# The last branch projection of a hybrid encoder block as seven half-size products per chunk of weights, its right factors made a stage earlier

## The chip, the cores and the metric

The kernel runs on one core of a Trainium2 chip. The metric is the device time in microseconds from the start to the end of one execution. TensorE is called PE here, VectorE DVE, ScalarE ACT, GpSimd POOL, SyncE SP, as the profile calls them.

## The reference, cut to what matters

One layer for two groups of tokens (256 and 512, together 768 columns) with the same weights. Three mixers (S5, differential attention, cross-attention) give three feature maps; each is projected by its own 1024x1024 matrix, gated and added; one output projection and a feed-forward network (FFN) follow.

```python
branches = jnp.stack([s5_out, diff_out.astype(x.dtype), mem_out.astype(x.dtype)], axis=2)
br = jnp.einsum('blnc,ncd->blnd', branches, w_branch[li])
gates = jax.nn.sigmoid((gl + b_gate[li]).astype(F32)).reshape(Bsz, L, N_BRANCH, D_MODEL)
merged = jnp.sum(gates * br.astype(F32), axis=2).astype(x.dtype)
x = x + merged @ w_out[li]
h2 = rmsnorm(x, ffn_norm_g[li])
g, up = jnp.split(h2 @ w_gate_up[li], 2, axis=-1)
x = x + (jax.nn.silu(g) * up) @ w_down[li]
```

The change concerns branch 1, the projection of the differential attention's output, and what is made ready for it.

## The kernel before, in words

Every float32 product is three matmuls in a reduced format (`mm3`, L748): each factor is split into a high part (ACT copies it and so rounds it) and a low part (factor minus high part, on DVE), and hi·hi, hi·lo and lo·hi are added in PSUM.

**Weights.** `WStream` (L518) streams all weights through fixed buffers: 3 raw halves of 512 KB (`wr`, loaded by SP), 4 high and 4 low tiles of 128x1024 (`wh`, `wl`). Weight block i is loaded in two halves `wr{i}_0` and `wr{i}_1`, and split while block i-1 is multiplied. A raw half is reused for the next load when all that reads it is done. For plain blocks the split is one copy on ACT (L595) and one subtraction on DVE (L601). Blocks of kind "w" (most of the FFN's gate and up weights) are split by `_split_w` (L561) for a product of 2x2 blocks in seven half-size products: POOL makes four sums S1 to S4 of the blocks A11, A12, A21, A22 of the weights (L572 to L579), and `_factor` (L547) makes the high and low parts of A11, A12, A22 and S1 to S4, 512 columns each, two factors to a tile. In one stretch of the program (L596 to L600) a low part is made without DVE: ACT writes the negated high copy and POOL issues a DMA that adds the raw weights to it (the "adding transfer").

**The stages around the change**, in the order in which they run: branch 2 (L1584), the half-GLU (L1587), branch 0 (L1618), branch 1 (L1620), output projection (`out_rows`, L1633), FFN. A branch runs over 4 chunks of 256 output channels (`branch`, L1505): weights 48 to 51 are branch 0, 52 to 55 branch 1 (its chunks 0 to 3), 56 to 59 the output projection. In a chunk there are 2 blocks of 128 channels (m) and 2 segments of tokens (256 and 512), each with 8 x 3 matmuls into a PSUM tile. Per m a gate row is loaded from DRAM by POOL (L1513) and goes through tanh on ACT (L1514); DVE multiplies PSUM by the gate (L1520) and adds it to `merged` (L1523). In branch 1 `merged` is then split into the pair `MG` (L1554, L1555), the left factor of the output projection.

The right factor of branch 1, the pair `Xd`, is loaded from DRAM (`br_scr`) and split by `load_pair` (L1561) during branch 0: eight rows, one 768-wide copy (L742) and one 768-wide subtraction (L743) each. The residual rows `x1` are loaded by POOL in branch 0 as well, from its second chunk on (`rows_in`, L1613). The output projection's PSUM tiles come from pools that are opened anew behind branch 1 (`psum`, L1622).

The source gives the instructions of all engines; the order of each engine's queue is set when the program is built, and an engine works its own queue strictly in that order.

## Time and profile before

| | us |
|---|---|
| time, median of 3 runs | 1745.99 (1744.87 to 1746.82) |
| profiled execution | 1746.11 |
| its span in the profile | 1744.3 |
| outside the span | 1.8 |
| branch 2, branch 0, branch 1: start to end on PE | 878 to 986, 1052.6 to 1119.9, 1119.9 to 1186.8 |
| output projection, from | 1186.8 |

Times in the trace are microseconds from the start of the span. A group row gives line, engine, operation, destination from sources, shape and count, then busy time and the mean of one in ns, then idle time of the engine in front of them and what ended it. A row of the windows gives start and end, length, busy time and instruction count of PE, PE's weight loads, DVE, ACT and POOL, the granted clock of PE, the share of DMA busy and GB/s. A DMA row gives destination from source, the issuing queue, count, size and median time from issue to landing.

### The profile page before, as it was taken

How to read it: one execution, taken by the hardware profiler on the slowest of the kernel's cores; microseconds unless marked ns; L12 is line 12 of the kernel's file. 1: busy time of each engine (PE TensorE's matmuls, PEld its weight loads, DVE VectorE, ACT ScalarE, POOL GpSimd, SP SyncE). 2: the span in 40 equal slices, each digit the busy share in tenths (PEclk: the TensorE clock that was granted, in tenths of full speed). 3: DMA queues.
4: the chain of work that ended last, by engine and by line, in shares of the span. 5: the costliest groups of instructions: out<-in, count | busy, mean ns of one | idle time of the engine just before them, and what ended most of it. 6: DMA issues, size and time to landing. Idle time of an engine off the chain costs nothing.

```text
span 1744.3 us, 29493 instructions
## 1 busy us (share of the span) xinstructions
PE 1731.5 (99%) x11236; PEld 1606.4 (92%) x11236; DVE 1262.6 (72%) x2353; ACT 889.4 (51%) x1868; POOL 270.1 (15%) x288
## 2 busy tenths in 40 slices
PE   9999999999999999999999999999999999999999
PEld 9999988999999999999989888888889999998887
DVE  7665749699999778887886445453598777776775
ACT  7444543776767346877775434232343333334443
POOL 0000000000000100111010002000036555541130
PEclk9999999999999999999999999999999999999999
DMA  8222736755566453745653437331312323238973
GB/s 271 74 85 91 125 120 134 187 126 141 145 158 159 122 145 93 169 91 155 169 160 106 133 116 247 118 118 61 90 62 91 109 91 109 91 110 290 252 158 96
DMA packets 209214, 234.11 MB, mean 134 GB/s; under 512 B 57832, under 2 KB 173296, under 8 KB 209072
## 3 DMA queue, kind: packets, MB, share of 16 engines
q1 hardware_dynamic: 182160, 167.49, 31.9%
q0 software_dynamic: 17440, 58.34, 15.5%
q10 hardware_dynamic: 9472, 6.39, 1.3%
q8 instruction: 89, 1.46, 0.4%
q14 instruction: 53, 0.43, 0.1%
HBM read 165.78 MB, written 41.22 MB: 119 GB/s over the span
## 4 chain that ended last, share of the span: by engine, by line
PE 96%; DVE 1%; ACT 1%; DMA 1%; issue 0%; SPq 0%; ACTq 0%; DVEq 0%
PE gl L751 4%; PE gl L753 4%; PE gl L752 4%; PE br L751 4%; PE br L752 4%; PE br L753 4%; PE gate L751 3%; PE gate L752 3%; PE up L752 3%; PE gate L753 3%; PE up L751 3%; PE up L753 3%; PE dn L753 3%; PE dn L751 3%; PE dn L752 3%; PE qk L751 3%
## 5 line engine op out<-in xcount | busy, mean ns | idle before, releaser
L595 ACT ACTIVATE wh<-wr 128x1024 fp32r<-128x1024 f32 x124 | 140.4, 1133 | 62.6 <-PE br L752 27.8
L601 DVE TENSOR_TENSOR wl<-wr,wh 128x1024 fp32r<-128x1024 f32 x82 | 108.5, 1324 | 80.8 <-ACT wh L595 79.0
L751 PE MATMUL gl<-H,wh 128*128 128x256 f32 (+1 forms) x384 | 132.2, 344 | 0.0
L753 PE MATMUL gl<-H,wl 128*128 128x256 f32 (+1 forms) x384 | 129.0, 336 | 0.0
L752 PE MATMUL gl<-H,wh 128*128 128x256 f32 (+1 forms) x384 | 128.7, 335 | 0.0
L599 POOL DMA_DIRECT2D wl<-wr x42 | 36.6, 872 | 506.1 <-ACT wl L598 486.8
L751 PE MATMUL qk<-wh,H 128*128 128x256 f32 x384 | 108.1, 282 | 0.0
L752 PE MATMUL qk<-wl,H 128*128 128x256 f32 x384 | 107.8, 281 | 0.0
L753 PE MATMUL qk<-wh,H 128*128 128x256 f32 x384 | 107.1, 279 | 0.0
L752 PE MATMUL dn<-wld,dxh 128*128 128x512 f32 x231 | 89.6, 389 | 0.0
L751 PE MATMUL dn<-whd,dxh 128*128 128x512 f32 x231 | 89.6, 389 | 0.0
L753 PE MATMUL dn<-whd,dxl 128*128 128x512 f32 x231 | 88.9, 389 | 0.0
L753 PEld LDWEIGHTS gl<-H,wl 128*128 128x128 f32 x384 | 72.0, 188 | 8.1
L752 PEld LDWEIGHTS gl<-H,wh 128*128 128x128 f32 x384 | 72.3, 188 | 7.2
L751 PEld LDWEIGHTS gl<-H,wh 128*128 128x128 f32 x384 | 72.3, 188 | 6.8
L557 ACT ACTIVATE wh_S<-ws 128x512 fp32r<-128x512 f32 x70 | 41.1, 625 | 65.2 <-PE up L752 36.8
L753 PEld LDWEIGHTS qk<-wh,H 128*128 128x128 f32 x384 | 72.4, 188 | 0.6
L751 PEld LDWEIGHTS qk<-wh,H 128*128 128x128 f32 x384 | 72.4, 188 | 0.6
L752 PEld LDWEIGHTS qk<-wl,H 128*128 128x128 f32 x384 | 72.3, 188 | 0.5
L558 DVE TENSOR_TENSOR wl_S<-ws,wh_S 128x512 fp32r<-128x512 f32 x70 | 57.9, 851 | 15.9 <-ACT wh_S L557 15.9
L1292 DVE TENSOR_REDUCE nm<-sc 128x1 f32<-128x512 f32 (+1 forms) x96 | 56.6, 596 | 17.6 <-PE sc L1287 16.8
L1294 ACT ACTIVATE p<-sc,nm 128x512 f32<-128x512 f32 (+1 forms) x96 | 58.8, 615 | 14.1 <-DVE nm L1292 13.6
(477 smaller groups left out, 6004.2 us busy)
## 6 DMA issues: line engine op xcount, KB each, us to landing
wr<-in_w_in_dram SPq DMA_DIRECT2D x48, 512.0 KB, 4.9
wr<-in_w_gate_up_dram SPq DMA_DIRECT2D x44, 512.0 KB, 3.6
wl<-wr POOLq DMA_DIRECT2D x42, 512.0 KB, 5.4
wr<-in_w_branch_dram SPq DMA_DIRECT2D x24, 512.0 KB, 4.8
glr<-gl_scr POOLq DMA_DIRECT2D x24, 384.0 KB, 4.0
hid_scr<-fa SPq DMA_DIRECT2D x11, 768.0 KB, 6.5
wr<-in_w_mem_kv_dram SPq DMA_DIRECT2D x16, 512.0 KB, 4.2
wr<-in_w_in_dram SPq DMA_DIRECT2D x32, 256.0 KB, 3.8
```

The lines of the kernel that those rows point to most:

```text
L557: self.nc.scalar.activation(f(hi), src, AF.Copy)
L558: self.nc.vector.tensor_tensor(out=f(lo), in0=src, in1=f(hi).bitcast(F32), op=ALU.subtract)
L595: self.nc.scalar.activation(hi, r, AF.Copy)
L599: self.nc.gpsimd.dma_start(lo, r.bitcast(F32R), accum_op=ALU.add)
L601: self.sub.tensor_tensor(out=lo, in0=r, in1=hi.bitcast(F32), op=ALU.subtract)
L751: pe.matmul(ps, wh, xh, start=start, stop=False, **kw)
L752: pe.matmul(ps, wh, xl, start=False, stop=False, **kw)
L753: pe.matmul(ps, wl, xh, start=False, stop=stop, **kw)
L1292: v.tensor_reduce(out=nm[:, m : m + 1], in_=ps, axis=AX.X, op=ALU.max, negate=True)
L1294: act.activation(pm[:, 0:n], ps, AF.Exp, bias=nm[:, m : m + 1], accum_out=s1s[:, tt : tt + 1] if m == 0 else s2)
```

## The change

- Weights 52 to 55 get a kind of their own, "w2": they are split as for seven products, with two sum buffers instead of three. S3 takes S1's buffer as soon as S1's parts are made, and S4 is written over S2. The low parts of A11 and A12 are made by adding transfers of 256 KB (four pieces of 512 bytes per partition), the others by DVE.
- The right factors B11, B21, B22 and T1 to T4 (differences of blocks of the branch's input; halves of the features by halves of the tokens) are made during branch 0: per step k two rows are loaded, DVE makes four differences, and six factors are split, 384 wide. T1 to T3 and the B's lie in the memory of `Xd` and of `x1`; T4 waits unsplit in a buffer of its own and is split into the last two rows of `MG` when branch 1 begins.
- So the loads of `x1` move from branch 0 to behind branch 1.
- Branch 1 runs `branch7`: per chunk seven products of 12 matmuls with 384 columns. A11·B11, S2·T2 and S3·T3 accumulate in one PSUM tile (the chain), which is copied out in between (c11, c12, c21); S1·T1 and S4·B22 share another. DVE adds the rest from PSUM to the results in SBUF, and gate, addition and split are 768 wide. In the last chunk the last two products and their merges are exchanged.

```diff
-    def _factor(self, i, key, src):
+    def _factor(self, i, key, src, by_dma=False):
...
         self.nc.scalar.activation(f(hi), src, AF.Copy)
-        self.nc.vector.tensor_tensor(out=f(lo), in0=src, in1=f(hi).bitcast(F32), op=ALU.subtract)
+        if by_dma:
+            self.nc.scalar.activation(f(lo), src, AF.Copy, scale=-1.0)
+            self.nc.gpsimd.dma_start(f(lo), src.bitcast(F32R), accum_op=ALU.add)
+        else:
+            self.nc.vector.tensor_tensor(out=f(lo), in0=src, in1=f(hi).bitcast(F32), op=ALU.subtract)
         self.parts.setdefault(i, {})[key] = f(hi), f(lo)
 
-    def _split_w(self, i, h):
...
-        self._factor(i, "A11", A11)
-        s1, s2, s3, s4 = (new(k) for k in range(4))
+        self._factor(i, "A11", A11, inplace)
+        s1, s2 = new(0), new(1)
+        if not inplace:
+            s3, s4 = new(2), new(3)
         gt(out=s1, in0=A21, in1=A22, op=add)
         gt(out=s2, in0=s1, in1=A11, op=sub)
-        self._factor(i, "A12", A12)
+        self._factor(i, "A12", A12, inplace)
         self._factor(i, "S2", s2)
         self._factor(i, "S1", s1)
+        if inplace:
+            s3, s4 = new(2), s2
         gt(out=s3, in0=A11, in1=A21, op=sub)
         self._factor(i, "S3", s3)
...
-        if kind == "w":
-            return self._split_w(i, h)
+        if kind in ("w", "w2"):
+            return self._split_w(i, h, kind == "w2")
...
-            W.add(cols(nme, 256 * c), 8, 256)
+            W.add(cols(nme, 256 * c), 8, 256, "w2" if nme == "w_branch1" else None)
...
-            L["x1"] = [xp.tile([128, 1024], F32, name=f"x1_{t}") for t in range(TILES)]
+            L["x1"] = xp
...
-        Xd = pair(XB, "xd")
-        load_pair(Xd, br_scr)
-
-        def rows_in(c):
-            if c == 1:
-                for t in range(TILES):
-                    tc.keep_in_program_order(gp.dma_start(x1[t], xs[t]))
-
-        branch(0, S, hook=rows_in)
...
+        W.sums = fctx.enter_context(tc.tile_pool(name="wsumb", bufs=2))
...
+        rc = xp.tile([128, 8, TOK], F32R, name="rc", tag="x1")
...
+        for k in range(4):
+            r0, r1 = (stg.tile([128, TOK], F32, name=uid("brr"), tag="brr") for _ in range(2))
+            gp.dma_start(r0, br_scr[k])
+            gp.dma_start(r1, br_scr[k + 4])
+            (b11, b12), (b21, b22) = ((r[:, h1], r[:, h2]) for r in (r0, r1))
+            put = lambda n_, src: split_evac(RB[n_][0][:, k], RB[n_][1][:, k], src)
+            put("B11", b11)
+            put("B22", b22)
+            put("B21", b21)
+            v.tensor_tensor(out=b11, in0=b12, in1=b11, op=sub)
+            v.tensor_tensor(out=b12, in0=b22, in1=b12, op=sub)
+            v.tensor_tensor(out=b22, in0=b22, in1=b11, op=sub)
+            v.tensor_tensor(out=t4[:, k], in0=b21, in1=b22, op=sub)
+            put("T1", b11)
+            put("T3", b12)
+            put("T2", b22)
+
+        branch(0, S)
         MG = rows_pair("mgd", 0)
-        branch(1, Xd, MG=MG)
+        RB["T4"] = tuple(t[:, 6:8].rearrange("p a (b t) -> p (a b) t", b=2) for t in MG)
+
+        def branch7(n_):
+            for c in range(4):
+                w = W.get()
+                if c == 0:
+                    for k in range(4):
+                        split_evac(RB["T4"][0][:, k], RB["T4"][1][:, k], t4[:, k])
+                gs = []
+                for m in range(2):
+                    g = gtp.tile([128, TOK], F32, name=uid("glr"), tag="glr")
+                    gp.dma_start(g, gl_scr[8 * n_ + 2 * c + m])
+                    act.activation(g, g, AF.Tanh, scale=0.5)
+                    gs.append(g)
+                cs = [stg.tile([128, TOK], F32, name=uid("bs"), tag="brr") for _ in range(2)]
+                (c11, c12), (c21, c22) = ((t[:, h1], t[:, h2]) for t in cs)
+                chain = env.psb("brc")[:, 0:HT]
+
+                def prod(l, r, ps=None, start=True):
+                    if ps is None:
+                        ps = psd("br")[:, 0:HT]
+                    (wh, wl), (xh, xl) = w[l], RB[r]
+                    for k in range(4):
+                        mm3(ps, wh[:, k], wl[:, k], xh[:, k], xl[:, k], start and k == 0, k == 3, not start)
+                    return ps
+
+                def plus(o, ps):
+                    v.tensor_tensor(out=o, in0=o, in1=ps, op=add)
+
+                def merge(m):
+                    M = 2 * c + m
+                    v.scalar_tensor_tensor(out=cs[m], in0=gs[m], scalar=1.0, in1=cs[m], op0=add, op1=mul)
+                    v.tensor_tensor(out=merged[:, M], in0=merged[:, M], in1=cs[m], op=add)
+                    act.activation(MG[0][:, M], merged[:, M], AF.Copy, scale=0.5)
+                    v.scalar_tensor_tensor(out=MG[1][:, M], in0=merged[:, M], scalar=0.5,
+                                           in1=MG[0][:, M].bitcast(F32), op0=mul, op1=sub)
+
+                act.activation(c11, prod("A11", "B11", chain), AF.Copy)
+                plus(c11, prod("A12", "B21"))
+                act.activation(c12, prod("S2", "T2", chain, False), AF.Copy)
+                p5 = prod("S1", "T1")
+                act.activation(c22, p5, AF.Copy)
+                prod("S3", "T3", chain, False)
+                plus(c22, chain)
+                act.activation(c21, chain, AF.Copy)
...
+                else:
+                    plus(c21, prod("A22", "T4"))
+                    merge(1)
+                    plus(c12, prod("S4", "B22", p5, False))
+                    merge(0)
+
+        branch7(1)
+        fctx.close()
+        x1t = xp.tile([128, TILES, 1024], F32, name="x1", tag="x1")
+        x1 = [x1t[:, t] for t in range(TILES)]
+        for t in range(TILES):
+            tc.keep_in_program_order(gp.dma_start(x1[t], xs[t]))
```

Line numbers of the changed kernel are 8 higher than before in `WStream` and some 90 higher behind the branches.

How this stands in the queues, at three places. First ACT, between the last products of one chunk of branch 1 and the first of the next (names: `wh54` is the high part of weights 54, `glr` a gate, `mgd` the pair MG). Before:

```order
L595 ACTIVATE wh54_0_13661<-wr54_0_13414 128x1024
L595 ACTIVATE wh54_1_13667<-wr54_1_13535 128x1024
L1554 ACTIVATE mgd_13530<-merged_11575 128x768
L1514 ACTIVATE glr_1491_13732<-glr_1491_13732 128x768
L1554 ACTIVATE mgd_13530<-merged_11575 128x768
L1514 ACTIVATE glr_1494_13803<-glr_1494_13803 128x768
L595 ACTIVATE wh55_0_13791<-wr55_0_13541 128x1024
L595 ACTIVATE wh55_1_13797<-wr55_1_13665 128x1024
```

In the changed program, from the copy of c12 of chunk 1 (`bs` is a result, `brc` the chain's PSUM tile, `ws` a sum) to the copies of c11 of chunk 2 and c21 of chunk 1:

```order
L1689 ACTIVATE bs_1490_13792<-brc_1492_13794 128x384
L557 ACTIVATE wh54_S3_13773<-ws541_13759 128x512
L557 ACTIVATE wh54_S3_13773<-ws542_13771 128x512
L557 ACTIVATE wh54_A22_13780<-wr54_1_13598 128x512
L557 ACTIVATE wh54_A22_13780<-wr55_0_13629 128x512
L559 ACTIVATE wl54_A22_13781<-wr55_0_13629 128x512
L557 ACTIVATE wh55_A12_13907<-wr55_1_13751 128x512
L559 ACTIVATE wl55_A12_13908<-wr55_1_13751 128x512
L1683 ACTIVATE mgd_13597<-merged_11575 128x768
L1687 ACTIVATE bs_1498_13937<-brc_1500_13939 128x384
L1694 ACTIVATE bs_1491_13793<-brc_1492_13794 128x384
```

Where two copies of whole tiles stood there are now seven half-size ones, one of them from the second raw half of weights 55, in front of the copy that frees the chain's tile.

Second POOL, in the second and third chunk of branch 1. Before, it only issues loads of gates:

```order
L1513 DMA glr_1485_13602<-gl_scr9_149 128x768
L1513 DMA glr_1488_13673<-gl_scr10_150 128x768
L1513 DMA glr_1491_13732<-gl_scr11_151 128x768
L1513 DMA glr_1494_13803<-gl_scr12_152 128x768
L1513 DMA glr_1497_13862<-gl_scr13_153 128x768
L1513 DMA glr_1500_13933<-gl_scr14_154 128x768
```

In the changed program, from s3 of weights 53 to the first adding transfer of weights 55 (L578 is S1, L579 S2, L585 S3, L587 S4, L560 the adding transfer; the tile `wl54_A22` holds A22 of weights 54 and A11 of weights 55):

```order
L585 TENSOR_TENSOR ws532_13618<-wr53_0_13332 128x512
L578 TENSOR_TENSOR ws540_13758<-wr54_0_13481,wr54_1_13598 128x512
L1661 DMA glr_1488_13786<-gl_scr10_150 128x768
L579 TENSOR_TENSOR ws541_13759<-ws540_13758,wr54_0_13481 128x512
L560 DMA wl54_A11_13754<-wr54_0_13481 128x4x128
L560 DMA wl54_A11_13754<-wr54_1_13598 128x4x128
L1661 DMA glr_1489_13789<-gl_scr11_151 128x768
L587 TENSOR_TENSOR ws541_13759<-wr54_1_13598,ws541_13759 128x512
L585 TENSOR_TENSOR ws542_13771<-wr54_0_13481 128x512
L1661 DMA glr_1496_13931<-gl_scr12_152 128x768
L578 TENSOR_TENSOR ws550_13903<-wr55_0_13629,wr55_1_13751 128x512
L560 DMA wl54_A22_13781<-wr55_0_13629 128x4x128
```

Sums, adding transfers and gates' loads now stand in one queue, and each waits for the one ahead.

Third DVE, at the end of branch 1 (weights 57 are the output projection's). Before:

```order
L1520 SCALAR_TENSOR_TENSOR glr_1503_13992<-glr_1503_13992,br_1504_13995 128x256
L1523 TENSOR_TENSOR merged_11575<-merged_11575,glr_1503_13992 128x256
L601 TENSOR_TENSOR wl57_0_14077<-wr57_0_13801,wh57_0_14076 128x1024
L1520 SCALAR_TENSOR_TENSOR glr_1503_13992<-glr_1503_13992,br_1505_14022 128x512
L1523 TENSOR_TENSOR merged_11575<-merged_11575,glr_1503_13992 128x512
L601 TENSOR_TENSOR wl57_1_14083<-wr57_1_13925,wh57_1_14082 128x1024
L1555 SCALAR_TENSOR_TENSOR mgd_13530<-merged_11575,mgd_13530 128x768
```

In the changed program, L1677 adds PSUM to a result, L1681, L1682 and L1684 are gate, addition and low part of MG:

```order
L1677 TENSOR_TENSOR bs_1506_14061<-bs_1506_14061,br_1510_14104 128x384
L1681 SCALAR_TENSOR_TENSOR bs_1506_14061<-glr_1504_14055,bs_1506_14061 128x768
L609 TENSOR_TENSOR wl57_0_14202<-wr57_0_13929,wh57_0_14201 128x1024
L1682 TENSOR_TENSOR merged_11575<-merged_11575,bs_1506_14061 128x768
L1677 TENSOR_TENSOR bs_1507_14062<-bs_1507_14062,brc_1508_14063 128x384
L609 TENSOR_TENSOR wl57_1_14208<-wr57_1_14047,wh57_1_14207 128x1024
L1684 SCALAR_TENSOR_TENSOR mgd_13597<-merged_11575,mgd_13597 128x768
L1677 TENSOR_TENSOR bs_1507_14062<-bs_1507_14062,br_1511_14132 128x384
```

The addition of the chain's tile (`brc_1508`), which the chain's last copy on ACT waits for, stands behind the low part of `wl57_0` and the addition to `merged`.

More of the change, by code (lines that the diff above doesn't have):

```diff
@@ L619, in get @@
         p = self.parts.pop(i)
-        if kind == "w":
+        if kind in ("w", "w2"):
             return p
@@ new lines, in hybrid_block @@
+        t4p = fctx.enter_context(tc.tile_pool(name="t4raw", bufs=1))
+        t4 = t4p.tile([128, 4, HT], F32, name="t4")
+        quarters = lambda t: [t[:, 2 * j : 2 * j + 2].rearrange("p a (b t) -> p (a b) t", b=2) for j in range(4)]
+        ra, rb = (XB.tile([128, 8, TOK], F32R, name="r" + n_, tag=tg) for n_, tg in (("a", "Xhi"), ("b", "Xlo")))
+        rc = xp.tile([128, 8, TOK], F32R, name="rc", tag="x1")
+        RB = {}
+        for t, ns in ((ra, ("B11", "B21")), (rb, ("B22", "T1")), (rc, ("T2", "T3"))):
+            q = quarters(t)
+            for j, n_ in enumerate(ns):
+                RB[n_] = q[2 * j], q[2 * j + 1]
@@ new lines, in hybrid_block @@
+        h1, h2 = slice(0, HT), slice(HT, TOK)
+        for k in range(4):
[14 more added lines that the diff above has]
+            put("T2", b22)
@@ new lines, in hybrid_block @@
+        branch(0, S)
+        MG = rows_pair("mgd", 0)
+        RB["T4"] = tuple(t[:, 6:8].rearrange("p a (b t) -> p (a b) t", b=2) for t in MG)
[38 more added lines that the diff above has]
+                act.activation(c21, chain, AF.Copy)
+                if c < 3:
+                    plus(c12, prod("S4", "B22", p5, False))
[3 more added lines that the diff above has]
+                else:
+                    plus(c21, prod("A22", "T4"))
+                    merge(1)
+                    plus(c12, prod("S4", "B22", p5, False))
+                    merge(0)
```

4 lines of the change are left out of this document (3 added, 1 removed).

## The prediction

> **What bounds the kernel now.** I read the page first: the span, the share of each engine, the chain that ended last.
>
> ```profile
> span 1744.3 us, 29493 instructions
> PE 1731.5 (99%) x11236; PEld 1606.4 (92%) x11236; DVE 1262.6 (72%) x2353; ACT 889.4 (51%) x1868; POOL 270.1 (15%) x288
> PE 96%; DVE 1%; ACT 1%; DMA 1%; issue 0%; SPq 0%; ACTq 0%; DVEq 0%
> ```
>
> TensorE (PE) is busy all but 12.8 us of 1744.3. So time can only come from fewer or shorter matmuls, and every wait that a change puts in front of PE is paid in full. Next the table of windows, one per stage: start and end, length, busy time by engine, clock, DMA share, GB/s.
>
> ```profile
> 1052.60:1119.90 67.30, 66.28 (x386) 58.13 (x385) 33.58 (x48) 22.96 (x27) 11.23 (x21) 1.00 0.59 197
> 1119.90:1186.80 66.90, 66.90 (x386) 59.23 (x385) 33.62 (x48) 19.99 (x22) 3.76 (x7) 1.00 0.33 105
> 1306.30:1320.90 14.60, 14.60 (x86) 14.60 (x86) 14.50 (x22) 5.96 (x12) 10.44 (x8) 1.00 0.25 72
> 1320.90:1582.00 261.10, 261.10 (x1508) 261.10 (x1507) 194.41 (x291) 99.27 (x180) 139.26 (x102) 1.00 0.34 110
> ```
>
> The rows are branch 0, branch 1, one FFN block that already runs by seven half-size products, and the other such blocks. Branch 1 has PE busy for all of its 66.90 us, VectorE (DVE) for half, ScalarE (ACT) for a third, GpSimd (POOL) almost idle. From branch 0 to the output projection the view of waits has one for PE, in branch 0 (waited for, us, times, longest):
>
> ```profile
> PE br L751 <- DVE glr L1520: 1.0, 1, 1.0
> ```
>
> **The change, part by part.** *The matmuls.* Branch 1 is now 384 matmuls of 256 or 512 columns; it becomes 4 chunks x 7 products x 12 = 336 of 384 columns. An FFN block has 84 of these in 14.60 us, 0.1738 each (261.10 / 1508 = 0.173 in the long row), so 336 x 0.1738 = **58.4 us, 8.5 less than 66.9**. The clock reads 1.00 in both rows. This is all the change can win here, and a wait in the new stage eats it.
>
> *What feeds the products.* These are the durations (busy, mean ns):
>
> ```profile
> L558 DVE TENSOR_TENSOR wl_S<-wr,wh_S 128x512 fp32r<-128x512 f32 x9 | 6.1, 679 | 0.0
> L1472 DVE TENSOR_TENSOR fs<-fs,up 128x384 f32<-128x384 f32 x5 | 2.6, 544 | 0.1
> L1555 DVE SCALAR_TENSOR_TENSOR mgd<-merged,mgd 128x768 fp32r<-128x768 f32 x7 | 6.7, 956 | 3.7 <-ACT mgd L1554 3.7
> L601 DVE TENSOR_TENSOR wl<-wr,wh 128x1024 fp32r<-128x1024 f32 x9 | 11.0, 1222 | 14.7 <-ACT wh L595 14.7
> L557 ACT ACTIVATE wh_S<-ws 128x512 fp32r<-128x512 f32 x64 | 37.6, 625 | 63.6 <-PE up L752 36.1 <-PE gate L752 23.5 <-POOL ws L579 4.0
> L1554 ACT ACTIVATE mgd<-merged 128x768 fp32r<-128x768 f32 x7 | 5.9, 846 | 12.4 <-DVE merged L1523 12.4
> L1478 ACT ACTIVATE fs<-up 128x384 f32<-128x384 f32 x10 | 4.8, 475 | 2.1 <-DVE fa L1432 1.4 <-PE up L753 0.7
> L595 ACT ACTIVATE wh<-wr 128x1024 fp32r<-128x1024 f32 x8 | 8.4, 1054 | 7.3 <-PE br L752 7.3
> L579 POOL TENSOR_TENSOR ws<-wr,ws 128x512 f32<-128x512 f32 x17 | 24.6, 1444 | 60.5 <-DVE wl_S L558 57.6 <-DMA wr<-in_w_gate_up_dram 2.9
> ```
>
> Behind one another on an engine they come a little faster than these busy times, since neighbours overlap by 0.05 to 0.1. Per chunk VectorE then has five low parts (0.68), four PSUM additions (0.54) and six 768-wide steps of the merges (0.95): 3.4 + 2.2 + 5.7 = 11.3 us of a chunk's 14.6. ScalarE has nine weight copies of 512 columns, four PSUM copies and four 768-wide ones: 5.6 + 1.9 + 3.4 = 10.9 us. GpSimd has four sums of 1.44 and four DMA issues. No engine is over PE's 14.6, so it is a matter of order, not of totals. The two DMAs and the loads:
>
> ```profile
> L599 POOL DMA_DIRECT2D wl<-wr x42 | 36.6, 872 | 506.1 <-ACT wl L598 486.8
> DMA to landing us min/median/max: 4.5/5.4/9.8
> dch<-in_w_down_dram POOLq DMA_DIRECT2D x15, 512.0 KB, 10.3
> glr<-gl_scr POOLq DMA_DIRECT2D x15, 384.0 KB, 4.0
> wr<-in_w_branch_dram SPq DMA_DIRECT2D x11, 512.0 KB, 4.1
> wr<-in_w_out_dram SPq DMA_DIRECT2D x6, 512.0 KB, 4.6
> x<-in_x_prompt_dram POOLq DMA_DIRECT2D x2, 512.0 KB, 6.8
> x<-in_x_sample_dram POOLq DMA_DIRECT2D x4, 512.0 KB, 9.1
> ```
>
> The first two rows are the adding transfer as it exists (512 KB, one piece per partition). The new one has 256 KB in four pieces per partition and no row of its own. Nearest from below: the median 5.4, from above the accumulating weight loads of the last stage (dch), 10.3. I take 5.4 to 6.4, since it moves half the bytes of the nearer row; half the bytes landing faster than 4.5 isn't excluded.
>
> *Branch 0.* Now the right factors of branch 1 are made here in eight copies and eight subtractions of 768:
>
> ```profile
> L742 ACT ACTIVATE xdhi<-brr 128x768 fp32r<-128x768 f32 x8 | 6.8, 846 | 8.7 <-DMA brr<-br_scr 8.5
> L743 DVE TENSOR_TENSOR xdlo<-brr,xdhi 128x768 fp32r<-128x768 f32 x8 | 7.6, 954 | 5.4 <-ACT xdhi L742 5.3
> ```
>
> After the change each of four steps has six copies on ScalarE and ten steps on VectorE, all 384 wide, about 0.48 each (the copy's row above; half of 954): 24 x 0.48 = 11.5 and 40 x 0.48 = 19.2, in place of 6.8 and 7.6. So ScalarE goes to 23.0 + 4.7 = 28 and VectorE to 33.6 + 11.6 = 45 of 67 us: hidden. Six loads of x1 leave GpSimd's queue there. The 1.0 wait can go, or become up to 2: I take -0.3. At the end of branch 1 the x1 loads land 6.8 to 9.1 us after they are issued behind the last product; the first addition of them stands behind 45 matmuls of 512 columns, 0.23 apart (below): 10.3. Nothing, with 1 to 3 us to spare.
>
> *The waits in branch 1.* I walk the queues in the new order, chunks 0 to 3, t = 0 at the first product; what starts at matmul n is due at 0.1738 n.
> - **A, low part of A11, chunk 2, n = 146, due 25.4.** s3 of chunk 1 waits for S1's low part, whose tile is free after matmul 52 (9.0): copy, subtraction, 10.3; s3 11.8; only then may the second half of chunk 2's raw weights load, 16.2; s1 17.7, a gate's DMA 18.2, s2 19.7; the adding DMA lands 25.1 to 26.1. Wait 0.5 (0 to 4).
> - **B, S2·T2 of chunk 2, n = 206, due 35.8.** It waits for the copy of c11, which is behind A12 of chunk 3 on ScalarE. That raw half waits for s3 of chunk 2: its tile is free at 25.2, behind a gate's tanh 26.5, two copies 27.7, low part 28.4, s4 and s3 on GpSimd 30.7, load 35.2. Then four ScalarE instructions (0.55, 0.55, 0.75, 0.45): 37.5. So from n = 206 on PE is 1.7 late (A and B together; 0 to 4).
> - **C, low part of A12, chunk 3, n = 242, due 42.1 + 1.7 = 43.8.** s1 waits for the same load: 36.7, A11's DMA 37.6, s2 39.1; A12's DMA lands 44.5 to 45.5. Wait 1.2 (0 to 4).
> - **D, S2·T2 of chunk 3, n = 300.** Its c11 copy on ScalarE is behind the tanh of a gate whose DMA waits for the merge of chunk 2; S4·B22 ends at n = 269: addition 0.55, merge step 0.95, issue and landing 4.0, tanh and copy 1.2: 6.7 us, where PE has 31 x 0.1738 = 5.4. Wait 1.3 (0 to 3).
> - **E, the output projection.** Its first matmul waits for the last copy of the chain (c21). The last `c22 += chain` is on VectorE behind a low part of w_out's weights and a 768-wide addition. The high part can be made 1.2 before the end and takes 1.05; low part 1.2, addition 0.95, c22 0.55, copy 0.45. About 2.8 after the last product (at least 0.54 + 0.48 = 1.0; 4 if the low part is later). Before there is none:
>
> ```profile
> 1186.63 0.39 PE L753 MATMUL br<-xdhi,wl 128*128 128x512 f32 x1
> 1186.86 0.39 PE L751 MATMUL wo<-wh,mgd 128*128 128x512 f32 x1
> ```
>
> A to E: 1.7 + 1.2 + 1.3 + 2.8 = 7.0. One more price comes from VectorE beside GpSimd; rows of the FFN block, in order of time and grouped:
>
> ```profile
> 1311.27 1.78 DVE L558 TENSOR_TENSOR wl_A<-wr,wh_A 128x512 fp32r<-128x512 f32 x1
> 1313.44 0.68 DVE L558 TENSOR_TENSOR wl_A<-wr,wh_A 128x512 fp32r<-128x512 f32 x1
> 1310.88 1.62 POOL L577 TENSOR_TENSOR ws<-wr 128x512 f32<-128x512 f32 x1
> ```
>
> ```profile
> L558 DVE TENSOR_TENSOR wl_S<-ws,wh_S 128x512 fp32r<-128x512 f32 x6 | 5.6, 954 | 0.0
> L558 DVE TENSOR_TENSOR wl_A<-wr,wh_A 128x512 fp32r<-128x512 f32 x2 | 2.5, 1230 | 0.0
> L558 DVE TENSOR_TENSOR wl_S<-wr,wh_S 128x512 fp32r<-128x512 f32 x1 | 1.3, 1305 | 0.0
> ```
>
> The same subtraction takes 1.78 beside a sum on GpSimd and 0.68 without one; PSUM additions stay at 0.54. The block's nine subtractions took 9.4 where 9 x 0.68 = 6.1: 3.3 for 10.44 us of GpSimd. In the chain of B and C lie two sums that a subtraction touches, 2.9 us: 0.9 more. **7.9 in all**. [...]
>
> **Sum.** 66.9 - 58.4 = 8.5 won, 7.9 given back, 0.3 from branch 0: 0.9 less than the profiled execution's 1746.1 (its span and 1.8 around it), **1745.2**. That execution stands 0.1 above the median 1745.99, so the change is 0.05%, which a measurement can't tell from nothing (0.2%, 3.5 us, is about what it can).
>
> **Rivals.**
> - *The feed keeps up.* The transfer lands at 4.5 or under, the loads too: A, B and C vanish, D halves (0.6), E is 2.6. Waits 3.2; 1746.1 - 8.5 + 3.2 - 0.3 = 1740.5. For it: the FFN blocks run seven products at 14.60 without a wait, with more sums on GpSimd. Against: they have no adding transfer, three sum buffers where the new stage has two, and the sums there are not made in place.
> - *The adding transfers land late (slower).* If they land like dch, at 10.3: the first one of chunk 1 is issued at 2.5 and due at 10.8, 2.0 late; A's then is issued at 21.2, lands 31.5, due 27.4: 4.1; B is covered; C's is issued at about 41.2, lands 51.5, due 48.2: 3.3; with D and E 13.5. 1746.1 - 8.5 + 13.5 - 0.3 = 1750.8. It decides (3.5 us slower, waits of 12.3) from a landing of about 9.9 on. For it: POOL's other accumulations. Against: none of the 42 adding transfers was above 9.8 and half were at 5.4 or under.
> - *VectorE becomes the bound (slower).* If every sum on GpSimd stopped VectorE for its whole length, as 1.78 beside 0.68 nearly is, a chunk would cost it 11.3 + 4 x 1.44 = 17.1, four 68.3, with E 71.1: 1746.1 + 71.1 - 66.9 - 0.3 = 1750.0. [...] Against it: the FFN block with 10.44 us of GpSimd pays 3.3, not 10.44, for it and keeps PE full.
>
> **Numbers.** The forecast case (waits of 4 to 12, that is 1741.3 to 1749.3) gets 0.40, the feed that keeps up 0.25, late transfers 0.25, VectorE as the bound 0.10. Forecast 1745.2, range 1739.5 to 1752: the lower end takes in the first rival, the upper one late transfers with an error of a microsecond; beyond lie 2 in 10. Within 0.2%: nearly all of the forecast case, 0.38. Faster by more: 0.27. Slower by more: 0.35.
>
> **What would show it.** In the changed profile: 336 products at 0.174 apart from waits; PE's waits named after the copy of c11 (B, D), the low parts by DMA (A, C) and the copy of c21 at the head of the output projection (E, 2.8); the new transfer's landing, 5 to 6.5; VectorE at about 45 us in branch 0. It is wrong if E is missing, if the transfer lands outside 4.5 to 7, or if PE waits in branch 0 for the right factors.

## The result, and the profile after

The changed kernel takes **1752.14 us** (median of 6 runs, 1751.4 to 1754.06) beside 1746.4 for the kernel before (6 runs, 1744.87 to 1747.8): a ratio of 1.0033, 95% interval 1.0023 to 1.0044. It is slower by 5.7 us. The forecast was 1745.2, a time that could not be told from no change, with a range to 1752.0: wrong in sign, and outside the range by 0.1.

The page of the changed kernel (its profiled execution took 1751.76, 1.8 of them outside the span):

```profile
span 1750.0 us, 29548 instructions
PE 1728.5 (99%) x11188; PEld 1608.6 (92%) x11188; DVE 1296.7 (74%) x2401; ACT 912.9 (52%) x1932; POOL 305.4 (17%) x312
```

PE has 48 matmuls fewer (11188 for 11236), but now stands still for 21.5 us of the span instead of 12.8. The windows: branch 0, branch 1, then three stretches of 15 us in branch 1 and at the head of the output projection.

```profile
1052.60:1119.74 67.14, 67.14 (x388) 59.03 (x388) 47.41 (x81) 28.54 (x48) 17.70 (x21) 1.00 0.51 151
1119.74:1190.94 71.20, 62.53 (x338) 60.60 (x336) 51.02 (x63) 39.19 (x67) 32.41 (x30) 0.95 0.56 131
1150.00:1165.00 15.00, 11.82 (x56) 11.29 (x55) 10.86 (x13) 9.12 (x17) 8.82 (x7) 0.83 0.53 119
1165.00:1180.00 15.00, 15.00 (x82) 14.73 (x81) 12.49 (x17) 6.79 (x11) 5.37 (x5) 0.94 0.58 152
1180.00:1195.00 15.00, 10.65 (x48) 9.45 (x48) 11.99 (x14) 8.27 (x12) 3.15 (x6) 0.89 0.58 203
```

Branch 1 takes 71.20 us where its window before had 66.90, and the clock column, 1.00 in all of this part before, falls to 0.83, 0.94 and 0.89. In the second of the three stretches PE is busy for all 15.00 us and still gets only 82 matmuls done (86 at 0.174). The waits of PE from branch 0 to the FFN:

```profile
PE brc L759 <- ACT bs L1687: 4.6, 2, 3.2
PE wo L759 <- ACT bs L1694: 2.9, 1, 2.9
PE br L759 <- DVE bs L1677: 0.7, 1, 0.7
PE br L759 <- ACT bs L1691: 0.4, 1, 0.4
```

The first row is the copy of c11 (3.2 in chunk 2, 1.5 in chunk 3), the second the copy of c21 in front of the output projection. From start to start of matmuls, less the 0.17 that one takes, PE stands 0.6, 0.9, 3.35, 1.6 and 3.05 us: 9.5. The timeline of PE at the two long waits (start, duration, then in brackets the idle time before and what ended it):

```profile
1157.25 0.34 PE L760 MATMUL brc<-ra,wh_A 128*128 128x384 f32 x1
1160.77 0.69 PE L759 MATMUL brc<-rc,wh_S 128*128 128x384 f32 x1 [3.18 <-ACT bs L1687]
1161.25 0.52 PE L760 MATMUL brc<-rc,wh_S 128*128 128x384 f32 x1
1161.57 0.52 PE L761 MATMUL brc<-rc,wl_S 128*128 128x384 f32 x1
...
1187.72 0.34 PE L761 MATMUL brc<-rc,wl_S 128*128 128x384 f32 x1
1190.94 0.79 PE L759 MATMUL wo<-wh,mgd 128*128 128x512 f32 x1 [2.88 <-ACT bs L1694]
1191.53 0.63 PE L760 MATMUL wo<-wl,mgd 128*128 128x512 f32 x1
1191.96 0.63 PE L761 MATMUL wo<-wh,mgd 128*128 128x512 f32 x1
```

Read the starts, not only the idle time. Behind the first wait the matmuls are 0.48 and then 0.32 apart instead of 0.17; the projection's are up to 0.59 and then 0.43 apart for 7 matmuls (3.13 us) where 0.23 is usual (1.6). Behind each of these two waits of 3 us PE was slow when it went on.

Where the 5.7 us come from, counted from first matmul to first matmul: branch 0 starts 0.17 later and is 0.56 shorter (66.65 for 67.21); branch 1 is 4.47 longer (71.20 for 66.73: 58.4 of matmuls, 9.5 of waits, so 3.3 that are neither); from the first projection matmul to the end it is 559.06 instead of 557.44, 1.62 more. Of the 3.3, 2.8 are the 18 slow matmuls behind the first long wait, and the rest is small; of the 1.62, 1.56 are the slow matmuls behind the second. The clock says the same: what is missing from 1.00, taken as a clock of 0.50, makes 15 x 0.17 / 0.5 = 5.1 us, 1.8 and 3.3, together 10.2 us at half speed. About 1.2 of these lie in the waits themselves; in the other 9 the matmuls, 0.32 apart for 0.17, lose the 4.4.

The chain that makes the 3.2 wait, in chunk 2, from the timeline of POOL:

```profile
1141.09 2.64 POOL L560 DMA_DIRECT2D wl_A<-wr  x2
1143.72 0.60 POOL L1661 DMA_DIRECT2D glr<-gl_scr  x1
1151.96 1.67 POOL L587 TENSOR_TENSOR ws<-wr,ws 128x512 f32<-128x512 f32 x1 [7.64 <-DVE wl_S L562]
1153.59 1.28 POOL L585 TENSOR_TENSOR ws<-wr 128x512 f32<-128x512 f32 x1
```

and from that of ACT:

```profile
1149.78 0.85 ACT L1662 ACTIVATE glr<-glr 128x768 f32<-128x768 f32 x1 [3.77 <-DMA glr<-gl_scr]
1150.53 1.14 ACT L557 ACTIVATE wh_S<-ws 128x512 fp32r<-128x512 f32 x2
1158.46 0.63 ACT L557 ACTIVATE wh_A<-wr 128x512 fp32r<-128x512 f32 x1 [1.36 <-DMA wr<-in_w_branch_dram]
1160.25 0.47 ACT L1687 ACTIVATE bs<-brc 128x384 f32<-128x384 f32 x1
```

The gate's load is issued on the same queue behind two adding transfers and lands 6 us later. ACT stands before its tanh for 3.77 us; behind the tanh stand the copies of S2 and S1; POOL's s4 and s3 wait for these parts, the last raw half of weights 55 waits for s3, and the copy of c11 stands on ACT behind the high part of that half.

DMA rows of the page and of the DMA view:

```profile
wl_A<-wr POOLq DMA_DIRECT2D x8, 256.0 KB, 5.0
x<-in_x_sample_dram POOLq DMA_DIRECT2D x4, 512.0 KB, 11.5
```

The adding transfer lands in 5.0 (the median of eight), at the lower end of the 5 to 6.5 that was forecast.

### The profile page after: what moved, and what is told of

Read it like the earlier page. It is cut to its first block, busy times and chain, and to the rows that moved or that the text cites. A ratio compares the mean times of both kernels' runs of the same rounds, so it can differ in the third digit from the quotient of the medians.

```text
span 1750.0 us, 29548 instructions
## 1 busy us (share of the span) xinstructions
PE 1728.5 (99%) x11188; PEld 1608.6 (92%) x11188; DVE 1296.7 (74%) x2401; ACT 912.9 (52%) x1932; POOL 305.4 (17%) x312
## 4 chain that ended last, share of the span: by engine, by line
PE 94%; DVE 2%; ACT 1%; DMA 1%; issue 1%; SPq 0%; POOL 0%; ACTq 0%; DVEq 0%
PE gl L759 4%; PE gl L761 4%; PE gl L760 4%; PE gate L759 3%; PE gate L761 3%; PE up L759 3%; PE up L761 3%; PE gate L760 3%; PE up L760 3%; PE dn L761 3%; PE dn L760 3%; PE dn L759 3%; PE br L759 3%; PE br L760 3%; PE br L761 3%; PE qk L761 3%
## 5 line engine op out<-in xcount | busy, mean ns | idle before, releaser
L603 ACT ACTIVATE wh<-wr 128x1024 fp32r<-128x1024 f32 x116 | 132.0, 1138 | 51.4 <-PE br L760 13.5
L609 DVE TENSOR_TENSOR wl<-wr,wh 128x1024 fp32r<-128x1024 f32 x74 | 98.8, 1336 | 63.0 <-ACT wh L603 61.2
L562 DVE TENSOR_TENSOR wl_S<-ws,wh_S 128x512 fp32r<-128x512 f32 x84 | 71.5, 873 | 36.5 <-ACT wh_S L557 31.9
L557 ACT ACTIVATE wh_S<-ws 128x512 fp32r<-128x512 f32 x84 | 49.6, 625 | 72.7 <-PE up L760 36.6
```

The costliest lines, as they stand in the source:

```text
L557: self.nc.scalar.activation(f(hi), src, AF.Copy)
L562: self.nc.vector.tensor_tensor(out=f(lo), in0=src, in1=f(hi).bitcast(F32), op=ALU.subtract)
L603: self.nc.scalar.activation(hi, r, AF.Copy)
L609: self.sub.tensor_tensor(out=lo, in0=r, in1=hi.bitcast(F32), op=ALU.subtract)
```

## The experiments

Two questions: is it the clock that makes 9.5 us of waits cost some 14, and what makes the waits? Theory: a wait of about 3 us halves the clock, and the waits come from the order on ACT and POOL and from the projection's PSUM tiles. Rivals: the slow matmuls have another cause (transfers, PSUM), and the adding transfers with their issues on POOL make the waits.

### The clock

**fill**: the changed kernel with 36 additional matmuls into an unused PSUM tile, at the places where PE waits.

```diff
+        def idle(n):
+            ps = env.psa("idle")[:, 0:HT]
+            for _ in range(n):
+                tc.keep_in_program_order(pe.matmul(ps, MG[0][:, 0, 0:128], MG[0][:, 0, 128:512], start=True, stop=True))
...
+                if c == 2:
+                    idle(19)
                 p5 = prod("S1", "T1")
...
+                if c == 3:
+                    idle(17)
```

> The changed kernel with 19 matmuls of 384 columns on data that lie ready, into an unused PSUM bank, in front of S1·T1 of chunk 2, and 17 behind the last product: they fill the two waits of 3.3 and 3.0 us, and nothing else is changed. Clock theory (a wait of 3 us halves the granted clock for the next 3 to 6 us): the clock stays at 1.00 from 1150 to 1195 us of the span, the 18 products and 7 output matmuls that ran at half clock take 0.174 and 0.227 again, and the time falls by 3.5 to 4.5 us to about 1748, although PE does 6.3 us more of work. Rival (the clock falls for another reason, by these products or by the transfers beside them): the clock falls as before and the time stays at 1752 or rises. If the waits are not of fixed end but move with PE, the time rises by up to 6 to 1758.

1750.83 us (1.0027, 1.0018 to 1.0037). The windows of the two places, and the waits:

```profile
1150.00:1165.00 15.00, 14.26 (x79) 13.53 (x79) 9.78 (x12) 9.10 (x16) 8.86 (x7) 1.00 0.46 114
1180.00:1195.00 15.00, 13.00 (x69) 12.10 (x70) 12.33 (x15) 8.21 (x13) 3.14 (x6) 1.00 0.62 200
```

```profile
PE brc L759 <- ACT bs L1692: 2.2, 1, 2.2
PE br L759 <- DVE bs L1682: 1.4, 2, 0.8
PE br L759 <- ACT bs L1698: 1.0, 1, 1.0
```

With PE kept busy at the long waits the clock stayed 1.00. Little of the time came back: the additional matmuls take 36 x 0.174 = 6.3 us themselves and the remaining gaps make 5.5, no less together than the 9.5 before. So the mechanism agrees, the size was missed. One wait of 2.2 was left (2.3 by the starts), and the clock stayed 1.00 behind it; waits of this length are compared below.

**bwait2**: the cleaner test, on the kernel *before*, whose branch 1 has no wait. Its last PSUM tile comes from the pool that the projection opens with, and two copies of it on ACT are added that nothing needs. **bwait0** is the same without the two copies.

```diff
-                        ps = psd("br")
+                        last = MG and c == 3 and m == 1 and sg == 1
+                        ps = env.psb("br") if last else psd("br")
...
+                        for _ in range(2 if last else 0):
+                            tc.keep_in_program_order(act.activation(g[:, c0 : c0 + n], ps[:, 0:n], AF.Copy))
```

> The kernel before, untouched but for a wait: the last PSUM tile of branch 1 comes from the pool over which the output projection's tiles are opened, and two further copies on ScalarE (into a gate buffer that is no longer read) read it, so PE waits some 3.5 us between branch 1 and the output projection. Clock theory: behind the wait the clock is 0.5 for 3 to 6 us, 7 to 14 of the output matmuls are 0.43 apart instead of 0.227, and the time rises by 5 to 6.5, more than the wait: 1751.5 to 1752.5. Rival (a wait costs its own length): clock 1.00, time + 3.5, about 1749.7.

> The kernel before with its last product of branch 1 in a bank that the projection's first matmuls don't need freed later, and only the ordinary copy behind it: the wait of the earlier probe without the two extra copies, about 0.9 us instead of 3.4. Theory (only a wait of about 3 us halves the clock): +0.9 to +1.2, 1746.3, granted clock 1.00 in every window. Rival (any wait there costs twice its length): +2 and over, with matmuls 0.43 apart behind it.

bwait2: 1752.15 beside 1745.44 (1.0035, 1.0023 to 1.0048), 6.7 us for one wait; by the starts of its matmuls 3.6 of standing still and 3.0 of 14 slow ones behind it. A price of 3.5 alone would be a ratio of 1.0020, just below the interval. Its window and its timeline of PE:

```profile
1180.00:1195.00 15.00, 11.59 (x45) 9.26 (x45) 6.41 (x8) 4.44 (x6) 0.00 (x0) 0.81 0.32 105
```

```profile
1189.93 0.80 PE L751 MATMUL wo<-wh,mgd 128*128 128x512 f32 x1 [3.41 <-ACT glr L1553]
1190.52 0.63 PE L752 MATMUL wo<-wl,mgd 128*128 128x512 f32 x1
1190.95 0.63 PE L753 MATMUL wo<-wh,mgd 128*128 128x512 f32 x1
```

bwait0: 1747.41 beside 1746.08 (1.0008, 0.9999 to 1.0017). Its wait and window:

```profile
PE wo L751 <- ACT wh L595: 0.9, 1, 0.9
```

```profile
1180.00:1195.00 15.00, 14.13 (x66) 11.48 (x65) 6.32 (x8) 3.15 (x4) 0.00 (x0) 1.00 0.28 105
```

The same place, no seven products, no adding transfer: a wait of 0.9 left the clock at 1.00 and cost 1.3 us by the medians (3.0 at most by the interval); a wait of 3.4 cost 6.7. The rivals for the slow matmuls fall.

### What makes the waits

**wo_banks**: the projection's PSUM tiles are taken in turn from two pools, so that its first ones lie in banks that branch 1 doesn't use.

```diff
-    psd = lambda n="d": PS["d"].tile([128, 512], F32, name=uid(n), tag="d")
+    def psd(n="d"):
+        k = "d"
+        if turn[0] >= 0:
+            k = "aaddd"[turn[0] % 5]
+            turn[0] += 1
+        return PS[k].tile([128, 512], F32, name=uid(n), tag=k)
...
-        psum(3, d=5, b=3)
+        psum(3, a=2, d=3, b=3)
+        turn[0] = 0
```

> The output projection's PSUM tiles come from two pools, the first of them in two banks that branch 1 doesn't use, so its first matmuls need not wait for the last copy of the chain; the order on PE then puts 24 of them between the last products. Order theory: the wait at the end (3.05) and the one on c11 of chunk 3 (1.6) go, and with the first also the half clock behind it (1.4): 1752.1 - 6 = 1746. The wait on c11 of chunk 2 and its half clock stay. Rival (VectorE and ScalarE are too late there anyway, the wait only moves to the next tile): less than 2 us are won, 1750 to 1752.

1745.52 (0.9997, 0.9988 to 1.0006), as expected. The waits in front of the projection and for c11 in chunk 3 are gone, since the program now puts projection matmuls between the last products; the 3.2 in chunk 2 stays, with a clock of 0.89 in its window. 6.3 us come back (by the two ratios). Of the 8.5, this one wait (3.4) and the slow matmuls behind it (1.4) still eat 4.8, and the two small waits of the first chunks 1.6.

**tanh_late**: the gate's tanh on ACT is put in the merge, behind the copy of c21.

```diff
-                    act.activation(g, g, AF.Tanh, scale=0.5)
...
+                    tc.keep_in_program_order(act.activation(gs[m], gs[m], AF.Tanh, scale=0.5))
                     v.scalar_tensor_tensor(out=cs[m], in0=gs[m], scalar=1.0, in1=cs[m], op0=add, op1=mul)
```

> The tanh of a gate is pinned behind the copy of c21 of its chunk on ScalarE, so weight copies no longer wait behind a gate's load; the order on PE changes with it. Order theory: S2 of chunk 2 is copied 3 us earlier, the wait of 3.35 us on c11 of chunk 2 shrinks to 0 to 1.5, the clock stays at 1.00 there: 4 to 6.5 us less, about 1747. Rival (the adding transfers and sums on GpSimd set the pace): the wait stays at 3 us or moves to the low parts of A11 and A12, time 1750 to 1753.

1748.95 (1.0014, 1.0005 to 1.0023). The waits:

```profile
PE brc L761 <- DMA wl_A<-wr: 2.4, 2, 2.2
PE br L759 <- ACT bs L1691: 2.1, 1, 2.1
PE brc L759 <- ACT bs L1687: 1.5, 1, 1.5
PE wo L759 <- ACT bs L1694: 1.4, 1, 1.4
```

The 3.2 for c11 in chunk 2 is gone, so it did hang on the tanh that waits for its gate; but in its place PE waits 2.2 for an adding transfer. One wait was in front of the other: the theory's wait went, the rival's came, and the time lies between the two.

**both** (tanh_late and wo_banks together):

> tanh_late and wo_banks together. Order and clock theory: no wait of over 2 us is left from 1119 to 1195 us of the span, the clock is 1.00 throughout, the time 1740 to 1743, below the kernel before (1746.4). Rival (GpSimd's chain sets the pace): 1746 to 1750.

1743.04 (0.9977, 0.9969 to 0.9986): faster than the kernel before, but just above the 1740 to 1743 of the theory: one long wait is left, 2.0 for an adding transfer, and behind it the clock is 0.50 for 3.4 us, where 1.00 was expected.

**wo_fill** (wo_banks, and 19 additional matmuls at the 3.2 wait):

> wo_banks with 19 matmuls of 384 columns on ready data in front of S1·T1 of chunk 2; they fill the wait of 3.2 us on c11 of chunk 2, the only long one that wo_banks had left. Clock theory: no half clock is left (in wo_banks 0.89 from 1150 to 1165), PE does 3.3 us more and the time falls by 0 to 2.5, 1743 to 1745.5; waits that move with PE (S1·T1 is later) can eat up to 2. Rival: the time rises by up to 3.3.

1744.67 (0.9991, 0.9982 to 1.0000), clock 1.00 everywhere, although 3.3 us of work that nothing needs were added.

**dve_low**: the low parts of A11 and A12 by DVE like the others; everything else of the change stays.

```diff
-        self._factor(i, "A11", A11, inplace)
+        self._factor(i, "A11", A11)
...
-        self._factor(i, "A12", A12, inplace)
+        self._factor(i, "A12", A12)
```

> The changed kernel with the low parts of A11 and A12 made by a subtraction on VectorE like the others: no adding transfers, two copies fewer on ScalarE and two DMA issues of 1.3 us fewer on GpSimd per chunk. Rival theory (the adding transfers and their issues on GpSimd make the waits): the wait on c11 of chunk 2 shrinks below 1.5 and the time falls by 3 to 6, to 1746 to 1749. Order theory (the raw load behind s3 and the tanh in front of the weight copies make it): the gate's load comes only about 2 us earlier, the wait shrinks to about 2, the time falls by 1 to 3; the wait at the end (3) stays.

**1741.54** (0.9969, 0.9958 to 0.9980), 11 us less than the changed kernel in the ratios, and better than either account expected. One wait is left in branch 1:

```profile
PE brc L761 <- DVE wl_A L562: 2.0, 1, 2.0
```

The links of the chain that were read above, in its timeline of POOL and then of ACT:

```profile
1143.15 0.55 POOL L1661 DMA_DIRECT2D glr<-gl_scr  x1 [4.11 <-DVE bs L1681]
1148.06 1.28 POOL L585 TENSOR_TENSOR ws<-wr 128x512 f32<-128x512 f32 x1
```

```profile
1146.58 0.85 ACT L1662 ACTIVATE glr<-glr 128x768 f32<-128x768 f32 x1
```

The gate's load is issued at the same time (1143.15 for 1143.72), but nothing stands ahead of it on its queue and the tanh begins 3.4 us later, without idle time before it, instead of 6.1; s3 comes at 1148.06 instead of 1153.59. But the program has changed ACT's order as well:

```profile
1145.00 1.15 ACT L557 ACTIVATE wh_S<-ws 128x512 fp32r<-128x512 f32 x2
```

The two copies of sums that stood behind the tanh in the change (1150.53) now stand ahead of it. They do so in tanh_late too, where both adding transfers are still issued ahead of the gate's load, and there the 3.2 wait is gone as well. So what is shown is that the wait hung on these copies standing behind a tanh that waits for its load. That the transfers make this load late is read from its times alone: no run takes the transfers away and leaves ACT's order as it was.

The end differs as well: the program now puts S3·T3 of the last chunk ahead of S4·B22, so that twelve matmuls hide the copy of c21, and the wait of the projection (3.05) is gone too. That part is the order that came with the edit, and was not separated from it.

**sums3**: the changed kernel with a third sum buffer for weights 54 and 55, so that s3 doesn't wait for the parts of S1.

```diff
-        t4p = fctx.enter_context(tc.tile_pool(name="t4raw", bufs=1))
+        t4ctx = fctx.enter_context(ExitStack())
+        t4p = t4ctx.enter_context(tc.tile_pool(name="t4raw", bufs=1))
...
+                if c == 1:
+                    t4ctx.close()
+                    W.sums = fctx.enter_context(tc.tile_pool(name="wsumc", bufs=3))
```

> The changed kernel with a third buffer for the in-place sums of the right weights, for the last two groups of chunks; nothing else. Theory (the 3.4 us wait for the copy of c11 in chunk 2 goes back to s3 standing behind the subtraction that reads S1's sum buffer, and so the raw load of A12 behind s3): s3 is made about 3 us earlier, the load with it, that wait shrinks to 0 to 1.5 and the granted clock stays 1.00 around it; about 1747. Rival (the adding transfers and the gate's tanh behind their issues set the wait): the wait for c11 stays at 3 us and over, time 1751 to 1752.

1749.89 (1.0020, 1.0010 to 1.0030): the theory's mechanism, but a time nearer to the rival's. Its timeline of POOL, and the waits:

```profile
1141.84 1.30 POOL L585 TENSOR_TENSOR ws<-wr 128x512 f32<-128x512 f32 x1
```

```profile
PE wo L759 <- ACT bs L1698: 2.9, 1, 2.9
PE br L759 <- DVE bs L1681: 2.1, 1, 2.1
PE brc L761 <- DMA wl_A<-wr: 1.1, 1, 1.1
PE brc L759 <- ACT bs L1691: 0.8, 1, 0.8
```

s3 is made 12 us earlier and the wait for c11 in chunk 2 (last row) falls from 3.2 to 0.8, with a clock of 1.00 there. Counted from the start of branch 1 the copy of c11 ends only 1.6 us earlier (39.4 for 41.0), and PE comes to it 0.8 later. The same time is waited elsewhere (2.1 for DVE in chunk 1, 1.1 for an adding transfer): gaps of 9.0 for 9.5. What is won, 2 us, is of the size of the half clock's price there (6.8 us of it, 2.8 lost), not of the wait's.

**both_dve** (dve_low, tanh_late, wo_banks), **dve_banks** (dve_low, wo_banks), **sums3_dve_banks** (that and the third buffer):

> tanh_late, wo_banks and dve_low together. Order theory: with the tanh and the output tiles out of the way, the transfer of A11 of chunk 3 (2.0 us late in both) is the last long wait; without it no wait of over 1 us is left, the clock is 1.00, and the time is 1739 to 1741.5. Rival (VectorE has no room for two more subtractions a chunk): PE waits for low parts on VectorE, 1742 to 1746.

> The changed kernel with the low parts of A11 and A12 subtracted on VectorE and with the projection's first tiles in banks that branch 1 doesn't use. If the two repairs are for different waits they add up only in part, since the subtraction alone had left one wait of 2.0: 1740.5 to 1742. Rival (the two overlap in full): the time of the subtraction alone or slightly more, 1741.5 to 1742.5, with one wait of about 2 us left in chunk 2.

> The same with the third sum buffer as well. If what is left (2 us in chunk 2) comes from s3 behind S1's buffer: no wait over 1 us, 1738.5 to 1740.5. Rival (it comes from the order on ScalarE and VectorE, which the buffer doesn't change): 1741 to 1742, a wait of 1.5 to 2.5 left.

1741.97 (0.9980, 0.9971 to 0.9989), 1740.33 (0.9970, 0.9958 to 0.9981) and 1741.59 (0.9972, 0.9962 to 0.9982): none can be told from dve_low alone. Each has one wait of 2.0 to 2.1 left, where chunk 2 gives way to chunk 3, in two of them as in dve_low for the low part of A11 of chunk 3 on DVE; the third buffer doesn't take it away and adds one of 0.8. So the rivals of the last two runs hold: the repairs overlap. One pair is worth a look, the window of the 2.0 wait in dve_low and then in dve_banks:

```profile
1150.00:1165.00 15.00, 13.00 (x66) 12.68 (x65) 12.72 (x16) 6.90 (x12) 7.22 (x5) 0.89 0.38 123
```

```profile
1150.00:1165.00 15.00, 13.00 (x75) 12.68 (x74) 13.23 (x16) 7.77 (x14) 7.21 (x5) 1.00 0.40 123
```

The same wait at the same matmul, PE busy 13.00 us in both: once the clock is halved and 66 matmuls are done, once it is not and there are 75. So the same wait cost its 2 us in one execution and, by 9 matmuls of 0.174 fewer, about 3.6 in the other (an estimate from these two rows).

How the two differ shows when the clock column is cut finer. In the change half clocks begin at 1159.90, 1190.62 and, behind its last matmul, 1750.42: 30.72 and 559.80 us apart, which is 9 and 164 times 3.413. The first two last 6.84 and 3.42 us, two and one times this length. So in this trace all of them begin, and the first two end, at points a whole multiple of 3.413 us apart; why, is not shown. In dve_low such a point is 1159.52, where its half clock begins; it ends at 1162.93. For dve_banks one is estimated from the half clock behind its last matmul, which begins at 1737.84, and from the change's distances (559.80 / 164 = 3.4134): 170 times that back lies about 1157.57. First dve_low, then dve_banks, cut at these points:

```profile
1156.11:1159.52 3.41, 1.41 (x8) 1.34 (x8) 3.41 (x5) 0.63 (x1) 1.37 (x2) 1.00 0.37 108
1159.52:1162.93 3.41, 3.41 (x12) 3.41 (x12) 3.41 (x5) 1.96 (x3) 1.68 (x2) 0.50 0.60 202
```

```profile
1154.16:1157.57 3.41, 2.22 (x13) 1.90 (x11) 3.41 (x2) 0.91 (x3) 3.33 (x3) 1.00 0.00 0
1157.57:1160.98 3.41, 2.60 (x15) 2.60 (x16) 3.41 (x6) 0.95 (x2) 0.10 (x1) 1.00 0.72 225
```

In dve_low one stretch between two points holds the whole gap, and PE is busy for 1.41 us of it; in the next stretch the clock is 0.50, though PE is busy throughout. In dve_banks a point cuts the gap into 1.4 and 0.8 us, and the clock stays 1.00. The gaps from 1119 to 1200 us in the kernels with a half clock there sort like this: in the 3.41 us ahead of each of the nine half clocks PE stood for 2.0 to 2.8 us (by the starts; 2.5 and 2.7 in the change, 2.3 in tanh_late, 2.0 in both_dve), and the second wait of 2.2 in tanh_late, from 1181.44 to 1183.68, behind which the clock stayed 1.00, is cut into 1.8 and 0.4 by the point at 1183.23, six times 3.413 behind the start of its half clock at 1162.75.

Each trace is one execution, and the same kernel can fall otherwise in the next: tanh_late took 1746.7 us in its fastest execution, with a mean clock of 1.000, and 1752.5 in its slowest, with 0.996.

### One account for all

Per profiled execution: gaps of PE in branch 1 and in front of the projection (starts, less 0.17 each), the time at half clock (what the clock is short of 1.00 in the 15-us windows, over 0.5), and what is left of the execution's time when the gaps, half of the time at half clock and the additional matmuls are taken off.

| kernel | profiled execution | gaps | at half clock | rest |
|---|---|---|---|---|
| the change | 1751.76 | 9.5 | 10.2 | 1737.2 |
| fill (6.3 added) | 1750.83 | 5.5 | 0 | 1739.0 |
| wo_banks | 1745.53 | 4.9 | 3.3 | 1739.0 |
| tanh_late | 1748.95 | 9.3 | 3.3 | 1738.0 |
| both | 1744.03 | 3.6 | 3.3 | 1738.8 |
| wo_fill (3.3 added) | 1743.27 | 2.7 | 0 | 1737.3 |
| dve_low | 1742.32 | 2.5 | 3.3 | 1738.2 |
| both_dve | 1741.97 | 2.3 | 3.6 | 1737.9 |
| sums3 | 1750.07 | 9.0 | 3.3 | 1739.4 |
| dve_banks | 1740.44 | 2.2 | 0 | 1738.3 |
| sums3_dve_banks | 1741.85 | 3.1 | 0 | 1738.8 |

Times from 1740 to 1752 come down to 1737.2 to 1739.4, and the forecast's own figure without any wait was 1746.1 - 8.5 = 1737.6. Without the clock's term they would run from 1737.3 to 1742.3. Gaps and clock explain the eleven kernels to about 2 us. (Half is a little much as a price of the half clock: for the change it makes 5.1, by the starts it is 4.4.)

## Why the prediction was wrong

- **The matmuls, 8.5 us less: right to about a microsecond.** The rest column is this term by itself, 1737 to 1739 for 1737.6.
- **The failed step is the sum, where a wait was priced at its own length.** "A to E" were added up as microseconds of standing still. The two waits of 3 us cost another 4.4 by the matmuls at half speed behind them (2.8 in branch 1, 1.6 behind it); bwait2 shows the same on the kernel before, 6.7 for 3.4. That is most of the 6.6 us between the forecast and the profiled execution; the waits themselves make 1.6 of it. With this term the forecast's own E of 2.8 alone would have been 1.4 to 3.0 dearer (what 3.4 or 6.8 us at half clock cost here), and the time 1747 to 1748. None of the three signs that were to show the forecast wrong came; the clock wasn't among them.
- **The waits, 9.5 for 7.9: the total a little small, its parts less good.** D (1.6 for 1.3) and E (3.05 for 2.8, where its own terms add up to 3.0) came where and as forecast. A and C, the low parts by DMA, did not come. Two small ones (0.6 and 0.9, for the copy of c22 and an addition on DVE, in the first two chunks) were not seen.
- **B, 3.35 for 1.7 with A: mis-sized at "behind a gate's tanh 26.5".** The tanh was taken to start at once; its gate's load stood behind two adding transfers (2.64 of issue, where one of 512 KB in one piece had 0.87), and the tanh began at 1149.78 - 1119.74 = 30.0 and ended at 30.9. What follows is late by about as much: s3 ended at 35.1 for 30.7, the c11 copy at 41.0 for 37.5. tanh_late, sums3 and dve_low break this chain, and the wait fell to none, 0.8 and none; how much of the lateness the transfers make stays open.
- **Branch 0, about nothing: right.** The 1.0 wait is gone, DVE has 47.4 for 45, ACT 28.5 for 28, and no wait came in; from its first matmul to that of branch 1 it is 0.56 shorter, where 0.3 was forecast.
- **The x1 loads: right.** They land in 5.4 and 11.5 where 6.8 and 9.1 were thought; of the 1.62 us behind the first projection matmul, 1.56 are the slow matmuls there, which leaves nothing for a wait.
- **The rivals.** Late transfers gave 1750.8, near the result, but for the wrong reason: 5.0 landing, and no wait for them. VectorE as the bound fell: 51.0 us of 71.2 in branch 1. It was slower in places beside GpSimd (a step of 0.95 took 3.00 at 1160.37, beside a sum there), without ending a wait. In dve_low it may make the one wait that is left: just ahead of it on VectorE a step of 0.95 took 2.05 and two low parts of 1.28 together took 2.35, both beside sums on GpSimd, 2.2 us more for a wait of 2.0; no run separates this.

## What to carry to other kernels

Price a wait of PE of 2 us or more at its length and, as in these runs, up to 3.0 us more. Look at the starts of the matmuls behind it, since they, not the idle column, carry the second part; in dve_low they became slow only 1.3 us after PE had gone on. Here half clocks came behind stretches of 3.41 us in which PE stood for 2.0 us or more, and the wait of 0.9 in bwait0 cost 1.3. When a transfer is moved to an engine that also issues other loads (here GpSimd), walk what is queued behind it, to the end: here a small load behind timely transfers came late (used 6.1 us after its issue, 3.4 in dve_low), and ACT stood for 3.77 us before it. A single repair can uncover the next wait, so add the repairs' gaps up from one account and not from their separate gains.

## What the runs showed of the hardware

- **Behind stretches of 3.41 us in which PE stood for 2.0 us or more, the granted clock of TensorE fell to 0.50.** From 1119 to 1200 us that was so for all nine half clocks, in eight kernels, with 2.0 to 2.8 us of standing still (in dve_low PE is busy for 1.41 of 3.41 us, and the clock is 0.50 in the next 3.41). Single gaps of 3.0 to 3.6 us (five, in four kernels) were always followed by one; of those of 2.1 to 2.4 four were (dve_low, both, both_dve, one of two in tanh_late) and five weren't (dve_banks, sums3_dve_banks, sums3, fill and the other in tanh_late, all with a clock of 1.00 around them); those of 0.6 to 1.7 never. In the change the half clocks begin 9 and 164 times 3.413 us apart and last 6.84 and 3.42 us. The 2.0 is read from this stretch of long matmuls: in sums3 a half clock begins at 908.92, among short matmuls, behind 3.41 us in which PE is busy for 2.18.
- **What a half clock costs.** The granted clock is 0.50 for 3.4 us, or for 6.8 behind the 3.35 of the change and in bwait2; there PE still stood for 0.7 us or more when the half clock had begun, in the others for 0.5 or less. Matmuls of 384 columns start 0.32 apart in it instead of 0.17, those of 512 columns 0.43 instead of 0.23. 3.4 us of it cost 1.4 to 1.7 us, 6.8 cost 2.8 to 3.0.
- **A DMA issue on GpSimd of 256 KB in four pieces per partition took 1.3 us** (2.64 for two), more than the 0.87 of 512 KB in one piece, while it landed no later (5.0 for 5.5). The gate's load that is issued behind two of them (at 1143.72 in the change) was used 5.4 to 6.2 us after its issue in five kernels (the change, fill, wo_banks, wo_fill, sums3); without them 3.4 to 4.2 (dve_low, dve_banks, sums3_dve_banks).
